# Head norms of a two-branch decoder layer: sums of squares by a transposing reduce on VectorE instead of one-row matmuls on TensorE

## The chip, the core and the metric

The kernel runs on one NeuronCore of one Trainium2 chip. The metric is the device time of one execution in microseconds (us). TensorE (PE) multiplies matrices into PSUM; VectorE (DVE), ScalarE (ACT) and GpSimd (POOL) do elementwise work; SyncE (SP) issues nearly all DMAs, in program order.

## The reference, cut to what matters

One layer on 2048 positions of width 1024, all in float32. A combined input projection feeds a short convolution branch (1024 channels, 8 heads of 128) and a gated linear recurrence (1024 channels, 16 heads of 64). The step that changes is the norm of each head:

```python
def headwise_rms_norm(y, n_heads, g):
    b, s, d = y.shape
    yh = y.reshape(b, s, n_heads, d // n_heads)
    yh = yh * lax.rsqrt(jnp.mean(yh * yh, axis=-1, keepdims=True) + RMS_EPS)
    return yh.reshape(b, s, d) * g
...
    xn = rms_norm(h, ln_g)
    proj = jnp.einsum('bsd,de->bse', xn, w_in)
    b_gate, c_gate, x_conv, g_conv, x_lru, g_lru = jnp.split(proj, splits, axis=-1)
    y_conv = headwise_rms_norm(short_conv_mixer(...), N_CONV_HEADS, conv_out_g) * silu(g_conv)
    y_lru = headwise_rms_norm(rg_lru_mixer(...), N_LRU_HEADS, lru_out_g) * silu(g_lru)
    h = h + jnp.einsum('bse,ed->bsd', jnp.concatenate([y_conv, y_lru], -1), w_out)
    return rms_norm(h, final_g)
```

## The kernel before, in words

**Steps.** Channels lie on the 128 partitions and positions along the free axis. Positions are done in two halves of 1024, `h` = 0 and 1. A half has 24 steps: for each of 8 blocks of 128 channels a step "l" (recurrence), "a" and "b" (convolution). I call three such steps a triple. Then come 16 output steps "o". A step multiplies a 2x2 block of matrices by seven products instead of eight, each split into a high and a low part: seven groups of 4 x 3 matmuls of 128x128 by 128x512, all from line 886 into `bank` tiles in PSUM. The left factors are the tiles `s`, seven of them deep (`sset`, bufs=7). The first half makes them from `w_in` and stores them in HBM (`sd<-s`); the second half loads them (`s<-sd`). The output steps' factors (`so`) are made during the second half by a side job, described below, and loaded later (`s<-so`).

**Order.** The order on each engine is the order of the program's text, in slots: a slot is one product group, `tick()` opens it, and `at(n, f)` queues `f` for n slots later. Every engine works through its own queue in order, and SP does too. Each DMA instruction of SP also waits until the DMA eight places ahead of it on SP has landed, since eight semaphores are used in turn; the order's rows on waits show it below.

**What finishes a block.** `finish` gets a block's output `y` (tile `r` of the recurrence, tile `t` of the convolution, 128x1024) and its gate `sil` (tiles `gl`, `gb`). It multiplies them and stores the product (`yd<-gl`, `yd<-gb`). For the norm, ACT squares `y` in place (line 579), ACT copies it to the high part `qh` (line 581), and DVE subtracts to get the low part `ql` (line 160, the helper `tt`). Three slots later `head_sums` gives PE four matmuls, for two runs of 512 positions and two parts, each with a 128x64 slice of `sel` that has ones in one or two columns: they add one block's sums over channels to one or two rows of `norm_ps`, a PSUM tile into which all 16 blocks of a half accumulate. I call these four a quad; there are 32 of them. After the last, `head_norms` takes the square root (ACT), the reciprocal (DVE), and stores the 24 rows for each run of 512 positions into `rsd` with two DMAs.

**Who reads it.** `load_z` loads `yd` (`raw<-yd`) and the factors spread over partitions (`zr<-rsd`), and DVE multiplies them (`raw<-raw,zr`). The output steps need it for all positions. The side job `jobs()` starts with the third triple of the second half and does it for six of the output factors: it loads, multiplies, and writes seven pieces `so` each; in between it also prepares sums of `w_out` (`traw<-in_w_out_dram`, `td<-traw`). It makes one piece per slot, where `may()` allows it:

```python
    def may():
        p = place[0]
        if 8 <= p <= 12:
            return False
        return hlc[0] < (2 if p >= 20 or p <= 2 else 4)
```

`hlc` counts how many of the four `hl` tiles are taken; `qh` and `ql` are two of them, from two slots behind a block's `finish` to seven behind it. `gl` and `gb` take turns in two buffers (`o2`): DVE can't write the next one before the store of the last but one has landed.

Of the kernel before, what the change touches and what calls it, by code (L numbers as in the profile page):

```python
# [38 lines left out]
def hymba_kernel(ctx: ExitStack, tc: tile.TileContext, x, xt, w_in, par, lamc, w_gate, w_out, final_g, out):  # L39
# [51 lines left out]

    sel = const.tile([P, 3 * R], F32R, name="sel")
    nc.gpsimd.memset(sel.bitcast(F32), 0.0)
    nc.gpsimd.memset(sel.bitcast(F32)[:, R:R + 1], 1.0)
    nc.gpsimd.memset(sel.bitcast(F32)[:64, 2 * R:2 * R + 1], 1.0)
    nc.gpsimd.memset(sel.bitcast(F32)[64:, 2 * R + KT:2 * R + KT + 1], 1.0)

    inv_hd = const.tile([R, 1], F32, name="inv_hd")
    nc.vector.memset(inv_hd, 1.0 / 64)
# [197 lines left out]
    def load_z(h, m, zr, wait):  # L297
        r = [piece("raw") for _ in range(4)]
        fs = []
        for i in range(2):  # L300
# [4 lines left out]
            for q in range(2):
                zz = r[2 * i + q].rearrange("p (k t) -> p k t", k=NB)
                zq = z2[:, q * C:(q + 1) * C] if zr else piece("zr")
                k0 = (1 - h) * KT + q * NB
                nc.sync.dma_start(zz, yd[c][b, :, k0:k0 + NB, :])
                zq = zq.rearrange("p (k t) -> p k t", k=NB)  # L310
                if h == 1:
                    nc.sync.dma_start(zq, rsd[c][b:b + 1, k0:k0 + NB, :].broadcast_to((P, NB, P)))
                else:
                    nc.sync.dma_start(zq[:64], rsd[c][b:b + 1, k0:k0 + NB, :].broadcast_to((64, NB, P)))
# [225 lines left out]
    def head_norms(h):  # L540
        rs = aux("hn")[:R]
        nc.scalar.activation(out=rs, in_=norm_ps[0], func=AF.Sqrt, scale=inv_hd, bias=eps[:R])
        at(1, lambda: nc.vector.reciprocal(out=rs, in_=rs))

        def store():
            for i in range(2):
                nc.sync.dma_start(rsd[2 * h + i].rearrange("b h t -> h b t"),
                                  rs[32 * i:32 * i + 3 * KT, :].rearrange("h (b t) -> h b t", b=NB))
# [4 lines left out]
    def head_sums(h, qh, ql, col, row):
        if norm_ps[1] == 0:
            norm_ps[0] = psn.tile([P, C], F32, tag="norm", name="norm_ps")[:R]
        for i in range(2):
            s0 = col - (32 * i + row)
            for q in (qh, ql):
                nc.tensor.matmul(norm_ps[0], sel[:, s0:s0 + R], q[:, i * C:(i + 1) * C],  # L559
                                 start=norm_ps[1] == 0, stop=norm_ps[1] == 8 * KT - 1)  # L560
# [4 lines left out]

    def finish(d0, h, kt, y, sil, gain, col, row):
        v = {}

        def f1():
# [7 lines left out]

        def f2():
            nc.scalar.activation(out=y, in_=y, func=AF.Square)
            v["qh"], = hl_tile("qh")  # L580
            nc.scalar.copy(v["qh"], y)
# [702 lines left out]
```

## Time and profile before

| | |
|---|---|
| time, median of 3 runs | 1418.91 us (1418.45 to 1420.51) |
| span of the profiled execution, first to last instruction | 1418.1 us (the page gives no other time for it) |
| TensorE busy, matmuls | 94%, 5732 |
| VectorE / ScalarE / GpSimd busy | 75% / 55% / 17% |
| granted TensorE clock, mean | 0.981 |
| DMA moved | 371.02 MB, mean 262 GB/s |

Matmuls are pipelined, so the duration of one is longer than its share of the stream: what it costs is the distance from its start to the next one's start. "Idle before, releaser" in a row tells how long the engine stood still and which instruction ended that. By stages: a prologue to about 107 us, the first half to about 600, the second half to about 1120, and the output steps to the end.

### The profile page before, as it was taken

The page shows a single profiled execution, that of the slowest core. Times are in us where ns is not written, and L with a number is a line of the kernel's source. Part 1 is how long each engine was busy: PE and PEld are TensorE (multiplying, and loading weights), DVE is VectorE, ACT ScalarE, POOL GpSimd, SP SyncE. Part 2 cuts the span into 40 slices and gives each one's busy share as a digit, 9 for nine tenths or more (in the row PEclk, how much of TensorE's full clock was granted, in tenths as well). Part 3 has the DMA queues.
Part 4 walks back from the last instruction along what each step waited for, and adds up shares of the span by engine and source line. Part 5 has one row for each costly group of instructions (what it writes and reads, how often), then busy time and mean ns, then how long its engine had stood idle before and what let it go on. Part 6 is the DMA issues. An engine that isn't in the chain of part 4 may idle for free.

```text
span 1418.1 us, 16977 instructions
## 1 busy us (share of the span) xinstructions
PE 1336.5 (94%) x5732; PEld 1072.3 (76%) x5732; DVE 1069.9 (75%) x1273; ACT 782.6 (55%) x1165; POOL 242.6 (17%) x159
## 2 busy tenths in 40 slices
PE   6989999999999997899998999998996999988997
PEld 5867777778777775677886878786874888867886
DVE  6778788898989989777767667665667647657885
ACT  7485757666566666375563645463656323343443
POOL 2104333433534430101000000101010000000000
PEclk9999999999999998999999999999997999999999
DMA  5147797898888865730899999998979998697643
GB/s 213 30 141 256 274 280 212 310 326 284 310 280 293 315 242 198 240 97 30 291 315 339 331 339 333 368 294 302 300 259 340 352 304 260 223 390 284 214 155 144
DMA packets 165191, 371.02 MB, mean 262 GB/s; under 512 B 17265, under 2 KB 52465, under 8 KB 165105
## 3 DMA queue, kind: packets, MB, share of 16 engines
q1 hardware_dynamic: 164816, 369.63, 76.3%
q8 instruction: 45, 0.74, 0.2%
q14 instruction: 42, 0.34, 0.1%
q10 hardware_dynamic: 288, 0.32, 0.1%
HBM read 224.45 MB, written 145.43 MB: 261 GB/s over the span
## 4 chain that ended last, share of the span: by engine, by line
PE 65%; DMA 13%; ACT 9%; DVE 8%; issue 3%; SPq 2%; POOL 0%; DVEq 0%; ACTq 0%; POOLq 0%
PE bank L886 60%; PE norm_ps L559 2%; DMA sd<-s 2%; ACT i L673 2%; ACT r L673 2%; PE gate L666 2%; DMA s<-so 2%; DVE s L160 2%; DVE tl L160 1%; DMA yd<-gl 1%; DMA zr<-rsd 1%; DVE traw L160 1%; DMA raw<-in_w_in_dram 1%; DMA traw<-in_w_out_dram 1%; DMA raw<-yd 1%
## 5 line engine op out<-in xcount | busy, mean ns | idle before, releaser
L886 PE MATMUL bank<-th,s 128*128 128x512 f32 x3608 | 1147.0, 395 | 41.5 <-DMA s<-so 9.8
L886 PEld LDWEIGHTS bank<-th,s 128*128 128x128 f32 x3608 | 685.3, 190 | 204.4 <-ACT u L1223 12.2
L886 PE MATMUL bank<-tl,s 128*128 128x512 f32 x1804 | 710.5, 394 | 6.3 <-DVE tl L160 6.0
L886 PEld LDWEIGHTS bank<-tl,s 128*128 128x128 f32 x1804 | 342.9, 190 | 81.4 <-DVE tl L160 10.4
L160 POOL TENSOR_TENSOR s<-raw,s 128x512 fp32r<-128x512 f32 x62 | 118.9, 1931 | 256.4 <-ACT s L197 180.2
L197 ACT CAST s<-raw 128x512 fp32r<-128x512 f32 x136 | 81.8, 616 | 59.6 <-PE bank L886 43.4
L1223 ACT COPY u<-bank 128x512 f32<-128x512 f32 x58 | 34.0, 587 | 141.3 <-PE bank L886 90.9
L160 DVE TENSOR_TENSOR s<-s,s 128x512 fp32r<-128x512 f32 x102 | 103.5, 1015 | 5.4 <-ACT s L197 5.4
L160 DVE TENSOR_TENSOR tl<-traw,th 128x512 fp32r<-128x512 f32 x102 | 70.0, 711 | 47.5 <-ACT th L454 29.1
L160 POOL TENSOR_TENSOR gb<-gb,sg 128x1024 f32<-128x1024 f32 x16 | 41.8, 2611 | 351.4 <-ACT sg L599 331.4
L160 DVE TENSOR_TENSOR s<-raw,s 128x512 fp32r<-128x512 f32 (+1 forms) x120 | 89.8, 771 | 9.9 <-ACT s L197 5.3
L1220 ACT COPY q<-bank 128x512 f32<-128x512 f32 x58 | 33.8, 583 | 79.2 <-PE bank L886 74.2
L160 DVE TENSOR_TENSOR raw<-raw,zr 128x512 f32<-128x512 f32 x64 | 49.6, 801 | 29.6 <-DMA zr<-rsd 29.6
L197 ACT CAST s<-s 128x512 fp32r<-128x512 f32 x102 | 62.8, 616 | 5.9 <-DVE s L160 5.9
L640 DVE SCALAR_TENSOR_TENSOR u<-xl,pt,u 128x1024 f32<-128x1024 f32 x48 | 64.5, 1344 | 0.8 <-ACT u L636 0.2
L1226 ACT COPY rr<-bank 128x512 f32<-128x512 f32 x58 | 33.9, 584 | 47.8 <-PE bank L886 47.7
L160 DVE TENSOR_TENSOR st<-u,st 64x1024 fp32r<-64x1024 f32 x32 | 52.0, 1626 | 1.0
L750 DVE SCALAR_TENSOR_TENSOR t<-p,pt,t 128x1024 f32<-128x1024 f32 x32 | 47.6, 1486 | 4.9 <-ACT t L747 4.1
L160 POOL TENSOR_TENSOR gl<-gl,sg 128x1024 f32<-128x1024 f32 x16 | 45.8, 2862 | 20.1 <-ACT sg L599 20.1
L160 DVE TENSOR_TENSOR ob<-bank,rr 128x512 f32<-128x512 f32 x18 | 12.2, 689 | 48.0 <-ACT rr L1226 48.0
L636 ACT ACTIVATE u<-xl,pt 128x1024 f32<-128x1024 f32 x16 | 19.9, 1245 | 46.8 <-DVE xl L160 46.8
L673 ACT ACTIVATE r<-gate,pt 64x512 f32<-64x512 f32 x64 | 43.8, 684 | 2.4 <-PE gate L666 1.8
(162 smaller groups left out, 1355.9 us busy)
## 6 DMA issues: line engine op xcount, KB each, us to landing
sd<-s SPq DMA_DIRECT2D x147, 512.0 KB, 4.8
s<-sd SPq DMA_DIRECT2D x147, 512.0 KB, 5.9
raw<-in_w_in_dram SPq DMA_DIRECT2D x108, 256.0 KB, 5.0
so<-so SPq DMA_DIRECT2D x42, 512.0 KB, 6.0
s<-so SPq DMA_DIRECT2D x42, 512.0 KB, 7.5
raw<-yd SPq DMA_DIRECT2D x64, 256.0 KB, 5.4
traw<-in_w_out_dram SPq DMA_DIRECT2D x56, 256.0 KB, 5.9
yd<-gl SPq DMA_DIRECT2D x32, 256.0 KB, 3.6
```

What stands on the lines that cost most here:

```text
L160: (eng or nc.vector).tensor_tensor(out=out, in0=a, in1=b, op=op)
L197: nc.scalar.copy(dst[i][0], val(i))
L559: nc.tensor.matmul(norm_ps[0], sel[:, s0:s0 + R], q[:, i * C:(i + 1) * C], start=norm_ps[1] == 0, stop=norm_ps[1] == 8 * KT - 1)
L636: nc.scalar.activation(out=v["u"], in_=o1[:, 1:1 + N2], func=AF.Identity, scale=lw[0], bias=pt[:, LB + k:LB + k + 1])
L640: nc.vector.scalar_tensor_tensor(out=v["u"], in0=o1[:, 1 + j:1 + j + N2], scalar=lw[j], in1=v["u"], op0=ALU.mult, op1=ALU.add)
L666: nc.tensor.matmul(ps[j], v["gw"][n][:, j, :], v["st"][j][:, sl], start=(n == 0), stop=(n == 1))
L673: nc.scalar.activation(out=g_[hi, sl], in_=v["ps"][j][src], func=AF.Sigmoid, bias=pt[src, bias + k:bias + k + 1])
L750: nc.vector.scalar_tensor_tensor(out=tcur["t"], in0=p[:, 2 + j:2 + j + N2], scalar=cw[j], in1=tcur["t"], op0=ALU.mult, op1=ALU.add)
L886: nc.tensor.matmul(bank, a[:, js], b, start=start and n == 0, stop=stop and n == 2, skip_group_check=more)
L1220: nc.scalar.copy(q1, bk["A"])
L1223: nc.scalar.copy(u2, bk["A"])
L1226: nc.scalar.copy(rr, bk["A"])
```

## The change: one reduce per block, four short matmuls per half

The high and low parts, and the quads, go. After the square, DVE adds over channels in one `tensor_reduce` with `apply_transpose`: it reads the 1024 positions of a block as 32 runs of 32, in steps of 32 elements, transposes each 32x32 square of channels and positions, and adds along what were 32 channels. For each block it writes 32 columns of one PSUM tile `sums`: partition 32g+a, column r has the sum over channel group g at position 32a+r. When 16 blocks are done, `head_norms` splits `sums` into a high and a low part (`rt`), and four matmuls of 128x96 by 128x256 join two groups (heads of 64) or four (heads of 128). Root and reciprocal work on 96x256 instead of 64x512. The layout of the result is another one, so 24 DMAs of 4 partitions store it, in place of 2. `rsd` is laid out by halves.

```diff
-R = 64
+R = 32
+NR = 3 * R
...
-    rsd = [dram.tile([NB, 3 * KT, P], F32, name=f"rsd{c}") for c in range(NC)]
+    rsd = [dram.tile([2, NB, 3 * KT, P], F32, name=f"rsd{h}") for h in range(2)]
...
+    sel = [const.tile([P, NR], F32R, name=f"sel{n}") for n in range(2)]
...
     def head_norms(h):
-        rs = aux("hn")[:R]
-        nc.scalar.activation(out=rs, in_=norm_ps[0], func=AF.Sqrt, scale=inv_hd, bias=eps[:R])
-        at(1, lambda: nc.vector.reciprocal(out=rs, in_=rs))
+        sm_ = sums[0]
+        rt, = hl_tile("rt")
+        rh, rl = rt[:, 0:C], rt[:, C:2 * C]
+        at(4, lambda: hl_done(1))
+        v = {}
+
+        def split():
+            nc.scalar.copy(rh, sm_)
+            tt(rl, sm_, rh.bitcast(F32), ALU.subtract)
+
+        def add():
+            v["ps"] = pss.tile([P, C], F32, tag="s", name="norm_ps")[:NR, 0:KT * R]
+            parts = [(n, q) for n in range(2) for q in (rh, rl)]
+            for m, (n, q) in enumerate(parts):
+                nc.tensor.matmul(v["ps"], sel[n], q[:, (1 - n) * KT * R:(2 - n) * KT * R],
+                                 start=m == 0, stop=m == 3)
+
+        def root():
+            v["rs"] = aux("hn")[:NR, 0:KT * R]
+            nc.scalar.activation(out=v["rs"], in_=v["ps"], func=AF.Sqrt, scale=inv_hd, bias=eps[:NR])
 
         def store():
-            for i in range(2):
-                nc.sync.dma_start(rsd[2 * h + i].rearrange("b h t -> h b t"),
-                                  rs[32 * i:32 * i + 3 * KT, :].rearrange("h (b t) -> h b t", b=NB))
+            for w in range(3):
+                k0 = (w + 1) % 3 * KT
+                for i in range(2):
+                    for b in range(NB):
+                        p0 = w * R + (i * NB + b) * 4
+                        nc.sync.dma_start(
+                            rsd[h][i, b, k0:k0 + KT, :].rearrange("k (q r) -> q k r", q=4),
+                            v["rs"][p0:p0 + 4].rearrange("q (k r) -> q k r", k=KT))
...
+        split()
+        at(2, add)
+        at(3, root)
+        at(4, lambda: nc.vector.reciprocal(out=v["rs"], in_=v["rs"]))
+        at(5, store)
-    def head_sums(h, qh, ql, col, row):
...
-        for i in range(2):
-            s0 = col - (32 * i + row)
-            for q in (qh, ql):
-                nc.tensor.matmul(norm_ps[0], sel[:, s0:s0 + R], q[:, i * C:(i + 1) * C],
-                                 start=norm_ps[1] == 0, stop=norm_ps[1] == 8 * KT - 1)
+    def head_sums(h, kt, y):
+        if summed[0] == 0:
+            sums[0] = psn.tile([P, 2 * KT * R], F32, tag="sums", name="sums")
+        nc.vector.tensor_reduce(out=sums[0][:, kt * R:(kt + 1) * R], in_=y.rearrange("p (a r) -> p r a", r=R),
+                                axis=mybir.AxisListType.X, op=ALU.add, apply_transpose=True)
...
-    def finish(d0, h, kt, y, sil, gain, col, row):
+    def finish(d0, h, kt, y, sil, gain):
...
-        def f2():
-            nc.scalar.activation(out=y, in_=y, func=AF.Square)
-            v["qh"], = hl_tile("qh")
-            nc.scalar.copy(v["qh"], y)
-
-        def f3():
-            v["ql"], = hl_tile("ql")
-            tt(v["ql"], y, v["qh"].bitcast(F32), ALU.subtract)
...
-        at(d0 + 2, f2)
-        at(d0 + 3, f3)
-        at(d0 + 6, lambda: head_sums(h, v["qh"], v["ql"], col, row))
-        at(d0 + 7, lambda: hl_done(2))
+        at(d0 + 2, lambda: nc.scalar.activation(out=y, in_=y, func=AF.Square))
+        at(d0 + 3, lambda: head_sums(h, kt, y))
```

The order on the engines, at three places. First DVE in a triple of the first half, where `r` and `t` are a block's output; before:

```order
L160 TENSOR_TENSOR gl<-bank,rr 128x512
L160 TENSOR_TENSOR ql<-r,qh 128x1024
L160 TENSOR_TENSOR s<-raw,s 128x512
...
L160 TENSOR_TENSOR raw<-raw 128x512
L160 TENSOR_TENSOR ql<-t,qh 128x1024
L160 TENSOR_TENSOR s<-s_2784,s 128x512
```

And after, at the same places:

```order
L163 TENSOR_TENSOR gl<-bank,rr 128x512
L586 TENSOR_REDUCE sums<-r 128x32
L163 TENSOR_TENSOR s<-raw,s 128x512
...
L163 TENSOR_TENSOR raw<-raw 128x512
L586 TENSOR_REDUCE sums<-t 128x32
L163 TENSOR_TENSOR s<-s_2734,s 128x512
```

The reduce stands exactly where the subtraction stood; nothing else moves on DVE in the first half.

Second, SP in the second half, from the third load of gate weights (`bd`, one in each triple) on; `so` is the side job's store, `traw` its load of `w_out`. Before:

```order
L612 DMA bd<-in_w_gate_dram 128x256
L575 DMA yd_86<-gb 128x4x128
L575 DMA yd_87<-gb 128x4x128
L218 DMA s<-sd_103 128x1024
L218 DMA s<-sd_104 128x1024 x6
L381 DMA traw<-in_w_out_dram 128x512 x4
L218 DMA s<-sd_104 128x1024
L218 DMA s<-sd_105 128x1024
L422 DMA so_120<-so 128x1024
L218 DMA s<-sd_105 128x1024
L422 DMA so_120<-so 128x1024
```

After:

```order
L626 DMA bd<-in_w_gate_dram 128x256
L385 DMA traw<-in_w_out_dram 128x512 x4
L600 DMA yd_86<-gb 128x4x128
L600 DMA yd_87<-gb 128x4x128
L426 DMA so_118<-so 128x1024
L221 DMA s<-sd_101 128x1024
L221 DMA s<-sd_102 128x1024
L426 DMA so_118<-so 128x1024
L221 DMA s<-sd_102 128x1024 x5
L426 DMA so_118<-so 128x1024
L399 DMA td_127<-traw 128x512 x4
```

With two `hl` tiles no longer taken, `may()` says yes more often, and the side job runs ahead. Counted over the order's rows from one load of `bd` to the next, second half, triple by triple:

| loads of `bd` | 3rd to 4th | 4th to 5th | 5th to 6th | 6th to 7th | 7th to 8th | from the 8th on |
|---|---|---|---|---|---|---|
| `so` stores, before / after | 7 / 9 | 7 / 9 | 7 / 8 | 7 / 7 | 7 / 7 | 5 / 0 |
| `traw` loads | 8 / 12 | 8 / 8 | 8 / 8 | 4 / 0 | 0 / 0 | not the job's |
| `td` stores | 8 / 8 | 8 / 12 | 8 / 8 | 4 / 0 | 0 / 0 | 0 / 0 |
| `raw<-yd` loads | 4 / 4 | 4 / 4 | 4 / 8 | 4 / 4 | 4 / 0 | not the job's |

Third, SP in the output steps, where the factors of the second half are stored. Before:

```order
L218 DMA s<-so_122 128x1024 x3
L547 DMA rsd_90<-hn 24x4x128
L547 DMA rsd_91<-hn 24x4x128
L819 DMA od_138<-xr 128x1024
L218 DMA s<-so_122 128x1024
L218 DMA s<-so_123 128x1024 x2
L309 DMA raw<-yd_86 128x512
L314 DMA zr<-rsd_90 64x512
```

After:

```order
L221 DMA s<-so_120 128x1024 x2
L572 DMA rsd_89<-hn 4x8x32 x24
L221 DMA s<-so_120 128x1024
L833 DMA od_136<-xr 128x1024
L221 DMA s<-so_120 128x1024
L221 DMA s<-so_121 128x1024 x2
L313 DMA raw<-yd_86 128x512
L318 DMA zr<-rsd_89 64x512
```

The same place with the waits of each row, after:

```order
L221 DMA s<-so_120 128x1024 [waits DMAHW4_49,PE_49]
L572 DMA rsd_89<-hn 4x8x32 [waits DMAHW5_49,DVE_49]
L572 DMA rsd_89<-hn 4x8x32 [waits DMAHW6_49]
L572 DMA rsd_89<-hn 4x8x32 [waits DMAHW7_49]
L572 DMA rsd_89<-hn 4x8x32 [waits DMAHW0_49]
...
L221 DMA s<-so_120 128x1024 [waits DMAHW5_49,PE_49]
```

The store has moved one slot ahead, and 24 DMAs take turns on eight semaphores, so each waits for the one eight places ahead; four loads `s<-so` and the loads of `yd` and `rsd` stand behind them.

More of the change, by code (lines that the diff above doesn't have):

```diff
@@ L89, in hymba_kernel @@
     nc.scalar.activation(out=warm, in_=eps, func=AF.Exp)
[L92 to L99, printed above, removed]
-    for i in range(2):
-        nc.vector.memset(inv_hd[32 * i:32 * i + KT, :], 1.0 / 128)
+    sel = [const.tile([P, NR], F32R, name=f"sel{n}") for n in range(2)]
+    for n in range(2):
+        nc.gpsimd.memset(sel[n].bitcast(F32), 0.0)
+    quarter = [ident[:, g * R:(g + 1) * R] for g in range(P // R)]
+    for w in range(2):
+        nc.gpsimd.tensor_tensor(out=sel[0][:, w * R:(w + 1) * R], in0=quarter[2 * w],
+                                in1=quarter[2 * w + 1], op=ALU.add)
+    nc.gpsimd.tensor_tensor(out=sel[1][:, 2 * R:], in0=sel[0].bitcast(F32)[:, 0:R],
+                            in1=sel[0].bitcast(F32)[:, R:2 * R], op=ALU.add)
+    inv_hd = const.tile([NR, 1], F32, name="inv_hd")
+    nc.vector.memset(inv_hd[:2 * R], 1.0 / 64)
+    nc.vector.memset(inv_hd[2 * R:], 1.0 / 128)
     hx = const.tile([P, KT, 4], F32, name="hx")
@@ L301, in load_z @@
             c, b = divmod(2 * m + i, NB)
-            assert c < 2 or normed
+            assert normed[c // 2]
+            rs_ = rsd[c // 2][c % 2]
             zz_, zq_ = [], []
@@ L311, in load_z @@
                 if h == 1:
-                    nc.sync.dma_start(zq, rsd[c][b:b + 1, k0:k0 + NB, :].broadcast_to((P, NB, P)))
+                    nc.sync.dma_start(zq, rs_[b:b + 1, k0:k0 + NB, :].broadcast_to((P, NB, P)))
                 else:
-                    nc.sync.dma_start(zq[:64], rsd[c][b:b + 1, k0:k0 + NB, :].broadcast_to((64, NB, P)))
+                    nc.sync.dma_start(zq[:64], rs_[b:b + 1, k0:k0 + NB, :].broadcast_to((64, NB, P)))
                     k0 += KT
-                    nc.sync.dma_start(zq[64:], rsd[c][b:b + 1, k0:k0 + NB, :].broadcast_to((64, NB, P)))
+                    nc.sync.dma_start(zq[64:], rs_[b:b + 1, k0:k0 + NB, :].broadcast_to((64, NB, P)))
                 fs.append(lambda zz=zz, zq=zq: tt(zz, zz, zq, ALU.mult))
@@ L534, in second_half @@
                 at(free.pop(1) - 7, lambda c=c, kt=kt: cols(c, kt))
-    norm_ps = [None, 0]
-    normed = []
+    normed = [False, False]
+    sums, summed = [None], [0]
     def head_norms(h):
-        rs = aux("hn")[:R]
-        nc.scalar.activation(out=rs, in_=norm_ps[0], func=AF.Sqrt, scale=inv_hd, bias=eps[:R])
-        at(1, lambda: nc.vector.reciprocal(out=rs, in_=rs))
-        def store():
-            for i in range(2):
-                nc.sync.dma_start(rsd[2 * h + i].rearrange("b h t -> h b t"),
-                                  rs[32 * i:32 * i + 3 * KT, :].rearrange("h (b t) -> h b t", b=NB))
-            normed.extend([h] * h)
-        at(3, store)
@@ L553, in head_sums @@
-    def head_sums(h, qh, ql, col, row):
-        if norm_ps[1] == 0:
-            norm_ps[0] = psn.tile([P, C], F32, tag="norm", name="norm_ps")[:R]
-        for i in range(2):
-            s0 = col - (32 * i + row)
-            for q in (qh, ql):
-                nc.tensor.matmul(norm_ps[0], sel[:, s0:s0 + R], q[:, i * C:(i + 1) * C],
-                                 start=norm_ps[1] == 0, stop=norm_ps[1] == 8 * KT - 1)
-                norm_ps[1] += 1
-        if norm_ps[1] == 8 * KT:
-            norm_ps[1] = 0
+        sm_ = sums[0]
@@ new lines, in head_norms @@
+        split()
[8 more added lines that the diff above has]
+                                axis=mybir.AxisListType.X, op=ALU.add, apply_transpose=True)
+        summed[0] += 1
+        if summed[0] == 2 * KT:
+            summed[0] = 0
```

6 lines of the change are left out of this document (3 added, 3 removed).

## The prediction

> **What bounds the kernel now.** I read the page's busy shares first, then windows cut at the triples, then the timeline of TensorE around one quad, then the waits, and last DMA and SP. Columns of a window: length, busy us and count for PE, PEld, DVE, ACT and POOL, granted clock, DMA share, GB/s.
>
> ```profile
> PE 1336.5 (94%) x5732; PEld 1072.3 (76%) x5732; DVE 1069.9 (75%) x1273; ACT 782.6 (55%) x1165; POOL 242.6 (17%) x159
> 436.50:499.10 62.60, 61.85 (x270) 49.67 (x269) 57.29 (x58) 40.51 (x59) 25.60 (x15) 1.00 0.85 296
> 580.50:710.80 130.30, 128.75 (x564) 104.55 (x563) 92.09 (x106) 75.89 (x102) 14.19 (x8) 1.00 0.51 168
> 710.80:778.40 67.60, 63.40 (x275) 50.45 (x274) 45.26 (x52) 33.17 (x45) 5.91 (x4) 1.00 0.97 328
> 778.40:844.60 66.20, 63.42 (x270) 50.58 (x269) 45.39 (x52) 33.39 (x45) 5.92 (x4) 0.97 0.95 335
> 844.60:909.30 64.70, 61.84 (x270) 49.69 (x269) 45.21 (x52) 33.47 (x45) 5.91 (x4) 1.00 0.98 343
> 909.30:972.20 62.90, 59.07 (x257) 47.11 (x256) 39.55 (x46) 31.47 (x42) 6.27 (x4) 1.00 0.97 323
> 972.20:1033.70 61.50, 61.24 (x269) 49.47 (x268) 38.98 (x44) 33.36 (x45) 6.79 (x4) 1.00 0.88 292
> 1033.70:1120.00 86.30, 75.46 (x304) 58.43 (x303) 58.30 (x71) 48.44 (x70) 8.18 (x4) 0.90 0.85 310
> ```
>
> The second row is a triple of the first half: PE is full, and DVE is nearly full, 57.3 of 62.6 us. In the second half the same triple takes 67.6 down to 61.5 us. Where it takes most, DMA is busy 0.95 to 0.98 of the time; where DMA is at 0.88, it takes least. So three limits lie close together: PE everywhere, DVE in the first half, DMA from 711 to 972 us.
>
> **Quads removed.** Columns from here on: start, duration, engine, line, instruction.
>
> ```profile
> 311.18 0.39 PE L559 MATMUL norm_ps<-qh,sel 128*64 128x512 f32 x1
> 311.41 0.39 PE L559 MATMUL norm_ps<-ql,sel 128*64 128x512 f32 x1
> 311.64 0.40 PE L559 MATMUL norm_ps<-qh,sel 128*64 128x512 f32 x1
> 311.88 0.39 PE L559 MATMUL norm_ps<-ql,sel 128*64 128x512 f32 x1
> 312.11 0.39 PE L886 MATMUL bank<-th,s 128*128 128x512 f32 x1
> L559 PE MATMUL norm_ps<-ql,sel 128*64 128x512 f32 x64 | 25.7, 402 | 6.6 <-DVE ql L160 6.6
> ```
>
> A quad holds PE's stream for 312.11 - 311.18 = 0.93 us, and 32 of them for 29.8 us. Besides, PE stood 6.6 us before quads until `ql` came. The eight new matmuls have half the columns: at half of 0.23 us each, an estimate from these rows, 0.5 us per half. If PE alone set the end, the kernel would gain 29.8 + 6.6 - 0.9 = 35.5 us. The stages give much of it back.
>
> **DVE: the reduce for the subtraction.** No row of the trace has a transposing reduce, nor an operand read in steps of 32 elements.
>
> ```profile
> L160 DVE TENSOR_TENSOR ql<-t,qh 128x1024 fp32r<-128x1024 f32 x16 | 22.8, 1422 | 0.0
> L160 DVE TENSOR_TENSOR ql<-r,qh 128x1024 fp32r<-128x1024 f32 x16 | 20.0, 1251 | 0.0
> L700 DVE TENSOR_TENSOR_SCAN r<-r,hl,u 128x1024 f32<-128x1024 f32 x8 | 18.8, 2350 | 0.2
> L543 DVE RECIPROCAL hn<-hn 64x512 f32<-64x512 f32 x2 | 6.7, 3334 | 0.0
> 320.62 1.76 DVE L160 TENSOR_TENSOR ql<-t,qh 128x1024 fp32r<-128x1024 f32 x1
> 306.19 1.22 DVE L160 TENSOR_TENSOR ql<-r,qh 128x1024 fp32r<-128x1024 f32 x1
> DVE xx L160 <- PE bank L886: 2.3, 1, 2.3
> DVE u L160 <- ACT i L673: 0.8, 1, 0.8
> DVE gb L160 <- ACT rr L1226: 0.7, 1, 0.7
> DVE gl L160 <- ACT rr L1226: 0.5, 1, 0.5
> DVE s L160 <- ACT s L197: 0.5, 1, 0.5
> PE bank L886 <- DVE tl L160: 5.8, 5, 4.0
> L581 ACT CAST qh<-t 128x1024 fp32r<-128x1024 f32 x16 | 16.8, 1051 | 0.7 <-PE norm_ps L559 0.3
> ```
>
> The low end is 1.2 us, the subtraction itself: one element after the other. The high end is twice the reciprocal's 3.3 us for 512 elements, 6.7 us. I take 2.35 us, the scan's: it is the nearest row of a 1024-element pass that is slower than plain streaming, and each element of the reduce lies 128 bytes from the last. The Trainium skill, "Advanced Engine Details and Errata", section Memory Cachelines, says that an access to another 16-byte line each time is penalised in SBUF; no run here shows it, and it gives no factor. Against it, the Trainium skill, "VectorE: DVE Perf Modes", section The perf-mode tier table, has `tensor_reduce` at the plain one-element rate; no run here shows it, and by it the sum would be that of the low end. I give the low end 0.4.
>
> In a triple of the first half two subtractions go (1.22 + 1.76 = 3.0 us) and two reduces come (4.7 us): DVE 57.3 + 1.7 = 59.0 us. Of DVE's 5.3 us idle, the 2.3 us for PE can go, while some 2 us of waiting for ACT's results stay (the four rows on waits for ACT). DVE then needs about 61.1 us, and PE 62.6 - 1.9 = 60.7. So DVE sets the triple: a gain of 1.5 us instead of 1.9. From 107 to 499 us, 6.3 triples, that is -9 us (bounds: -12 to -15 with a 1.2 us reduce, where DVE needs 58.7 us and its last waits for PE's sake go too; 0 with one of 3.15 us). At the turn of the halves, 499 to 580 us, PE waits 5.8 us for weights `tl` that DVE splits, with a `ql` in that chain: three quads gained, 2.8 us, two longer reduces lost, 2.2 us: -0.5 us.
>
> ACT loses 32 casts of 1.05 us (line 581). I cost that at nothing: ACT is busy 40.5 of 62.6 us in the triple, so it mostly waits.
>
> **Second half: the side job runs ahead.** From 580 to 711 us DMA has room (0.51): four quads, -3.7 + 0.5 = -3 us. Then the change moves DMA work forward. The GB/s times the lengths give 22.2 MB in each of the three windows from 710.8 to 909.3 us.
>
> ```profile
> so<-so SPq DMA_DIRECT2D x42, 512.0 KB, 6.0
> traw<-in_w_out_dram SPq DMA_DIRECT2D x56, 256.0 KB, 5.9
> raw<-yd SPq DMA_DIRECT2D x64, 256.0 KB, 5.4
> DVE gl L160 <- DMA yd<-gl: 31.4, 6, 6.3
> 835.14 0.69 DVE L160 TENSOR_TENSOR gl<-bank,rr 128x512 f32<-128x512 f32 x1 [6.26 <-DMA yd<-gl]
> ```
>
> By the counts of the order, two `so` and four `traw` (or `td`) are added in the first and in the second of them, 2.1 MB each, and one `so` with a whole `load_z` (about 2.1 MB) in the third, 2.6 MB: 66.5 MB become 73.3. The last two rows show how a busy DMA reaches PE: the store of `gl` lands late, DVE stands 6.3 us for its buffer, and what is queued behind it, bank evacuations too, comes late. At the mean rate of the three windows, 335 GB/s, 73.3 MB take 219 us, against 198.5 now; at the rate of the best one with the share raised from 0.98 to 1.03, 360 GB/s, 203 us. If the added bytes were hidden, 198.5 - 5.6 for six quads - 3 for waits on `ql` = 190 us. I take 204.5: +6 us (bounds -9 and +14). Afterwards the work is missing: the window from 909.3 comes down to about PE's 60, the next one too: -2.9 - 1.5 = -4.5 us. From 1033.7 to 1120 us:
>
> ```profile
> PE bank L886 <- DMA s<-so: 7.1, 4, 2.9
> ```
>
> Three quads, -2.8; five `so` stores fewer, 2.6 MB or 8 us of DMA at 310 GB/s, in the place where PE waits for `s<-so`: I take -4 of the 7.1 us (bounds 0 and -7).
>
> **24 stores instead of 2.**
>
> ```profile
> L547 SPq DMA_DIRECT2D rsd<-hn x4: 312/338/363, 602.4 to 1129.4; - x4
> s<-so SPq DMA_DIRECT2D x42, 512.0 KB, 7.5
> 1129.06 0.73 SPq L547 DMA_DIRECT2D rsd<-hn  x2
> 1130.58 5.71 SPq L218 DMA_DIRECT2D s<-so  x3
> 1136.38 0.38 SPq L309 DMA_DIRECT2D raw<-yd  x1
> 1136.85 0.46 SPq L314 DMA_DIRECT2D zr<-rsd  x1
> ```
>
> On SP 24 issues at about 0.37 us (two in 0.73) are 9 us. With eight in flight, the first wait for big loads ahead to land (7.5 us), and two more rounds follow: 9 to 14 us before SP goes on. Behind them stand four `s<-so` and the `zr<-rsd` that need these stores. A tile `s` is reloaded six groups, 6 x 2.7 us = 16 us (12 matmuls of 0.23 us each group), before its use: 14 us late plus 7.5 us to land overshoots by some 5, 9 us late by nothing. I take +3 us in the output steps (bounds 0 and +12), with 0.5 for the short matmuls. At 602 us the window around it has DMA at 0.51, and I take 0.
>
> **Sum.** -9 - 0.5 - 3 + 6 - 4.5 - 6.8 + 3.5 = -14 us against the profiled span of 1418.1 us; the median, 1418.91, is 0.8 us above it, so about 1405. DVE's waits on ACT, 2.5 us in a triple, may shrink with ACT's shorter queue, for which I take off 2 in all: 1403 us. A difference of 0.2% (2.8 us) is about what can be told from none here.
>
> **Rivals.** (1) *The transfers are hidden anyway.* The second half's middle takes 190 us: 15 us less, 1388. For it: single stretches with big packets do move more than the 335 GB/s mean. Against it: the share of 0.95 to 0.98 over 200 us, and triples that get shorter as DMA gets freer. Chance 0.2. (2) *The stores take the place of the quads.* SP stands 14 us while DMA is busy, DVE waits for `zr`, PE for banks: +12 instead of +3, 1412 us. For it: the in-order queue; against it: the 16 us of lead. Chance 0.1. (3) *VectorE becomes the bound and the kernel is slower.* A triple of the first half takes 56.3 us + two reduces. It reaches today's 62.6 at 3.15 us; since the other stages gain 4 us, or 0.6 per triple, the kernel is slower from 3.5 us on. At the reciprocal's price of 6.7 us a triple takes 69.7: 6.3 x 7.1 = 45 us lost, less the 4: about 1460. For it: DVE's 57 of 62.6 us; against it: an addition does no division. Chance 0.08. (4) *It does nothing*: DMA gives back +14 and the stores +8 at once, 1416 to 1421 us. Chance 0.07. The forecast itself has 0.55, between 1395 and 1411.
>
> Eight times in ten the time lies between 1387 and 1416: this holds the forecast and the rivals (1) and (2). Faster by over 0.2%: the forecast, (1), (2), less a little for its tail, 0.84; same 0.08; slower 0.08.
>
> **What would show it.** Right: no row of line 559 but eight short matmuls; the reduce at 2.2 to 2.5 us; triples of the first half near 61 us with DVE over 58 busy; the three windows after 711 us at a DMA share near 1.0 and not shorter than now; 1034 to 1120 us shorter by 5 or more. A reduce near 1.2 us would give triples of about 60.2 us and 3 to 6 us more gain. Wrong: DMA at 0.95 with triples at 61 us there (rival 1), or a hole in PE of over 5 us just after the 24 stores (rival 2).

## The result, and the profile after

The changed kernel takes 1406.68 us (median of 4, 1404.29 to 1412.66) against 1418.68 us for the kernel before on the same chip: a ratio of 0.9914, 95% interval 0.9888 to 0.994. So it is faster, by 0.6 to 1.1%; the forecast was 1403 us. The profiled execution took 1404.29 us and has a span of 1402.2 us. A second set of five runs gave 1402.94 us (1398.37 to 1405.47), 0.9883 [0.9867, 0.9899]. The changed kernel scatters by 7 to 8 us between executions. Every ratio in this document is against the kernel before on the same chip, whose medians there lie between 1418.7 and 1419.9 us, so times from different chips can be compared to about 1 us.

First the busy shares, then the costliest groups that are new, from the page and the groups by line (behind the first bar: busy us and mean ns of one; behind the second: idle us before them):

```profile
PE 1309.4 (93%) x5612; PEld 1056.3 (75%) x5612; DVE 1071.1 (76%) x1274; ACT 749.3 (53%) x1135; POOL 225.9 (16%) x160
L586 DVE TRANSPOSE_TENSOR_REDUCE sums<-t 128x32 f32<-128x1024 f32 x16 | 33.8, 2110 | 0.0
L586 DVE TRANSPOSE_TENSOR_REDUCE sums<-r 128x32 f32<-128x1024 f32 x16 | 33.4, 2090 | 0.0
L559 PE MATMUL norm_ps<-rt,sel 128*96 128x256 f32 x8 | 1.3, 282 | 0.0
```

PE lost 120 matmuls, 27 us of busy time and the 6.6 us of waits for `ql`. ACT lost 33 us. DVE kept its 1070 us. The reduce costs 2.1 us. Of PE's 34 us, 16 reached the end of this execution (12 by the medians).

To see where, I cut both traces at events that are the same work in both: ACT's row `T<-r,nklam`, once per triple; the first `ob<-bank,q` of the output steps; the first `ob<-ob,rs,fg`, seven output steps later. Columns as in the prediction's windows. Before:

```profile
91.67:532.66 440.99, 431.80 (x1871) 346.28 (x1871) 390.73 (x393) 293.68 (x429) 168.97 (x101) 1.00 0.83 281
532.66:615.85 83.19, 68.53 (x265) 51.24 (x265) 63.73 (x80) 46.69 (x66) 6.72 (x4) 0.92 0.60 209
615.85:738.61 122.76, 122.40 (x537) 99.61 (x537) 87.20 (x101) 72.09 (x100) 14.14 (x8) 1.00 0.56 181
738.61:936.01 197.40, 187.57 (x805) 149.76 (x805) 135.76 (x154) 100.29 (x133) 17.76 (x12) 0.99 0.97 337
936.01:1108.67 172.66, 157.91 (x660) 124.57 (x660) 115.28 (x137) 96.95 (x132) 17.73 (x9) 0.95 0.87 300
1108.67:1285.71 177.04, 168.41 (x726) 137.76 (x725) 107.74 (x150) 56.24 (x97) 0.00 (x0) 0.98 0.90 309
1285.71:1418.07 132.36, 125.19 (x548) 103.22 (x546) 102.44 (x151) 56.95 (x111) 0.00 (x0) 0.98 0.56 185
```

After:

```profile
91.53:527.35 435.82, 421.27 (x1816) 340.88 (x1815) 383.04 (x393) 279.43 (x414) 154.10 (x101) 0.99 0.84 284
527.35:608.16 80.81, 65.81 (x261) 49.97 (x261) 64.31 (x81) 44.85 (x66) 6.69 (x4) 0.92 0.59 209
608.16:728.83 120.67, 119.49 (x521) 97.13 (x521) 95.07 (x108) 69.16 (x97) 12.55 (x8) 1.00 0.58 201
728.83:929.58 200.75, 185.53 (x782) 148.74 (x781) 145.12 (x164) 95.22 (x130) 18.65 (x12) 0.97 0.97 355
929.58:1087.25 157.67, 149.46 (x641) 120.56 (x641) 106.34 (x120) 87.41 (x121) 16.02 (x9) 0.99 0.86 290
1087.25:1271.24 183.99, 170.01 (x728) 137.40 (x727) 107.69 (x151) 56.50 (x98) 0.00 (x0) 0.98 0.86 297
1271.24:1402.23 130.99, 123.57 (x546) 101.98 (x544) 102.41 (x151) 56.97 (x111) 0.00 (x0) 0.99 0.56 187
```

The stages are: seven triples of the first half; the turn; two triples before the side job; three with it at its densest ("the middle"); the rest of the second half; seven output steps; the end. The sizes foreseen are for the prediction's own cuts (107, 499, 580, 711, 909 and 1120 us), so they fit these stages only roughly.

| stage | before | after | second profile of after | foreseen |
|---|---|---|---|---|
| first half | 441.0 | 435.8 (-5.2) | 433.4 (-7.6) | -9 |
| turn | 83.2 | 80.8 (-2.4) | 82.0 (-1.2) | -0.5 |
| two triples | 122.8 | 120.7 (-2.1) | 121.0 (-1.8) | -3 |
| middle | 197.4 | 200.8 (+3.4) | 200.4 (+3.0) | +6 |
| rest of the second half | 172.7 | 157.7 (-15.0) | 156.8 (-15.9) | -11.3 |
| seven output steps | 177.0 | 184.0 (+7.0) | 180.8 (+3.7) | +3.5 |
| end | 132.4 | 131.0 (-1.4) | 131.0 (-1.4) | 0 |

Read alone, this table confirms the prediction almost line by line. The experiments show that two of its lines are right for a wrong reason.

### The profile page after: what moved, and what is told of

Same layout as the page of the kernel before. It is cut to its first block, busy times and chain, and to the rows that moved or that the text cites. A ratio compares the mean times of both kernels' runs of the same rounds, so it can differ in the third digit from the quotient of the medians.

```text
span 1402.2 us, 16765 instructions
## 1 busy us (share of the span) xinstructions
PE 1309.4 (93%) x5612; PEld 1056.3 (75%) x5612; DVE 1071.1 (76%) x1274; ACT 749.3 (53%) x1135; POOL 225.9 (16%) x160
## 4 chain that ended last, share of the span: by engine, by line
PE 43%; DMA 19%; DVE 14%; ACT 6%; issue 6%; SPq 2%; POOL 1%; DVEq 0%; ACTq 0%; POOLq 0%
PE bank L900 42%; DMA s<-so 3%; DMA zr<-rsd 3%; DVE s L163 3%; DMA sd<-s 3%; DMA yd<-gl 2%; DVE sums L586 2%; PE gate L680 2%; ACT i L687 2%; ACT r L687 1%; DMA traw<-td 1%; DMA so<-so 1%; DVE u L654 1%; DMA raw<-in_w_in_dram 1%; DMA s<-sd 1%
## 5 line engine op out<-in xcount | busy, mean ns | idle before, releaser
L163 POOL TENSOR_TENSOR s<-raw,s 128x512 fp32r<-128x512 f32 x62 | 110.3, 1791 | 251.3 <-ACT s L200 221.1
L163 DVE TENSOR_TENSOR s<-s,s 128x512 fp32r<-128x512 f32 x102 | 88.9, 871 | 7.9 <-ACT s L200 7.9
L163 DVE TENSOR_TENSOR s<-raw,s 128x512 fp32r<-128x512 f32 (+1 forms) x120 | 85.0, 731 | 10.0 <-ACT s L200 5.3
L163 DVE TENSOR_TENSOR raw<-raw,zr 128x512 f32<-128x512 f32 x64 | 44.5, 721 | 29.7 <-DMA zr<-rsd 29.6
L654 DVE SCALAR_TENSOR_TENSOR u<-xl,pt,u 128x1024 f32<-128x1024 f32 x48 | 62.3, 1297 | 2.0 <-ACT u L650 1.5
L163 DVE TENSOR_TENSOR st<-u,st 64x1024 fp32r<-64x1024 f32 x32 | 45.5, 1422 | 1.0
L680 PE MATMUL gate<-st,bh 128*128 128x512 f32 x64 | 28.9, 452 | 16.7 <-DVE st L163 6.8
L687 ACT ACTIVATE i<-gate,pt 64x512 f32<-64x512 f32 x64 | 43.8, 684 | 1.1
```

The lines of the kernel that those rows point to most:

```text
L163: (eng or nc.vector).tensor_tensor(out=out, in0=a, in1=b, op=op)
L654: nc.vector.scalar_tensor_tensor(out=v["u"], in0=o1[:, 1 + j:1 + j + N2], scalar=lw[j], in1=v["u"], op0=ALU.mult, op1=ALU.add)
L680: nc.tensor.matmul(ps[j], v["gw"][n][:, j, :], v["st"][j][:, sl], start=(n == 0), stop=(n == 1))
L687: nc.scalar.activation(out=g_[hi, sl], in_=v["ps"][j][src], func=AF.Sigmoid, bias=pt[src, bias + k:bias + k + 1])
```

## Experiments: the pace of the side job

**The changed kernel again**, as the control for the runs beside it.

> The changed kernel once more, beside the next three on the same chip. All theories: 1404 to 1410 us, output steps of the first sixteen-row block 184 us long from the first to the second phase.

1402.94 us, as told above (span 1396.3): a little under what was expected, and with 180.8 us for the output steps instead of 184.

**The old pace.** By pace I mean how many pieces the side job makes in each triple. `may()` is the only link between the removed `hl` tiles and the order on SP. So the count alone is put back:

```diff
         at(d0 + 3, lambda: head_sums(h, kt, y))
+
+        def take(n):
+            hlc[0] += n
+
+        at(d0 + 2, lambda: take(1))
+        at(d0 + 3, lambda: take(1))
+        at(d0 + 7, lambda: take(-2))
```

> The changed kernel, with the count of taken hl tiles raised and lowered in the slots where qh and ql used to be taken, so that the side job keeps its old pace; nothing else differs. Theory (DMA is the limit in the middle of the second half, and the side job that runs ahead ate the gain): the three triples after 711 us go from 200.7 us to 188-193, the stretch from 909 us to the output steps, 157.7 us now, gets 6 to 10 us longer, total 1402 to 1409. Rival (the transfers are hidden, the 200.7 us have another cause, such as the granted clock of 0.95 there): the three triples stay at 199 to 202 and the later stretch at 157 to 160, total 1404 to 1409.

1424.00 us (1417.77 to 1431.12), 1.0037 [1.0022, 1.0052]: 21 us slower than the changed kernel, and slower than the kernel before. Neither theory gave this. The middle and the rest of the second half:

```profile
725.16:929.56 204.40, 187.79 (x781) 150.56 (x781) 137.23 (x154) 93.88 (x127) 18.40 (x12) 0.96 0.93 326
929.56:1105.69 176.13, 154.84 (x641) 122.00 (x640) 118.89 (x137) 90.63 (x126) 16.39 (x9) 0.95 0.85 294
```

The middle has no quads, moves the bytes that it moved before, and takes 204.4 us: not the 188 to 193 of my theory, and 7 us more than with the quads. The rest of the half takes 176 us, 20 more than at the new pace. So the side job that runs ahead did not eat the gain; it is where the gain is. The DMA share of 0.93 to 0.97 did not mean that DMA could do no more: at the new pace the middle moves 355 GB/s instead of 326 to 337, in less time than here.

**PE alone.** The kernel before, with only the last block's quad of each half; 15 of 16 blocks are left out of the sums.

```diff
+        if norm_ps[1] < 8 * KT - 4:
+            norm_ps[1] += 4
+            return
-        if norm_ps[1] == 0:
+        if norm_ps[1] == 8 * KT - 4:
...
```

> The kernel before, with the quad of the last block of each half alone: 30 of 32 quads are left out, and so the sums of 15 of 16 blocks; casts, subtractions, pace of the side job and stores stay. It relieves PE and nothing else. Theory (three limits close together): triples of the first half 62.6 to 60.5-61.2 us, the three triples after 711 us from 197.4 to 192-197 since DMA holds them, total 1395 to 1404. Rival (PE alone sets the end): all 28 us of the quads and 6 us of waits for ql are gained, 1383 to 1389.

1412.54 us, 0.9948 [0.9934, 0.9962]: 7 us for 30 quads that hold PE's stream for 28: neither theory had so little. Its steady triple of the first half, where 62.6 us should have become 60.5 to 61.2, and its windows of the middle and the rest of the second half:

```profile
406.09:468.37 62.28, 60.40 (x262) 48.41 (x261) 57.42 (x58) 40.49 (x59) 25.41 (x15) 1.00 0.86 298
732.29:933.28 200.99, 186.47 (x782) 149.56 (x781) 132.03 (x154) 100.13 (x133) 17.73 (x12) 0.97 0.96 331
933.28:1106.19 172.91, 155.40 (x642) 123.25 (x641) 115.33 (x137) 96.83 (x132) 17.02 (x9) 0.94 0.86 300
```

When the middle starts, it is 6.3 us ahead of the kernel before (732.3 against 738.6), the old-pace kernel 13.4 us (725.2). When the output steps start, the three stand at 1108.7, 1106.2 and 1105.7 us. At the old pace, then, what is gained ahead of the side job is nearly all lost in it; taking PE's work out there gained nothing in these executions.

The rows show part of the reason. In the middle this kernel has 23 matmuls fewer than the kernel before, but PE's busy time falls by 1.1 us only, not by 5, and the granted clock is 0.97 instead of 0.99. One quad of the middle, before:

```profile
770.78 0.45 PE L559 MATMUL norm_ps<-ql,sel 128*64 128x512 f32 x1 [1.43 <-DVE ql L160]
775.84 0.50 PE L886 MATMUL bank<-th,s 128*128 128x512 f32 x1 [1.40 <-ACT q L1220]
767.00:780.00 13.00, 10.18 (x44) 7.59 (x43) 10.96 (x14) 3.83 (x4) 0.00 (x0) 1.00 0.97 353
```

And the same place without the quad:

```profile
770.51 0.80 PE L889 MATMUL bank<-th,s 128*128 128x512 f32 x1 [3.18 <-ACT q L1223]
770.20:773.60 3.40, 3.09 (x7) 2.49 (x8) 3.36 (x4) 2.02 (x3) 0.00 (x0) 0.51 0.89 309
```

Before, PE stands 1.43 us for `ql`, does the quad, stands 1.40 us for `q`, and the granted clock stays at 1.00. Without the quad it stands 3.18 us at once, and goes on at half the clock. This happens once in each triple of the middle (3.14 to 3.18 us; 3.98 to 4.01 us in the old-pace kernel). So the quads there stood inside a wait that is no shorter without them. That the longer stop brings the lower clock is read from the order of events; no run tests it by itself.

**What holds the triples at the old pace.** In these 350 us DVE waits for the store of a block's product to leave the buffer of `gl`: in the old-pace kernel 29.0 us in five waits. (Rows on waits give us in all, times, longest.) One triple of it, SP and DVE:

```profile
DVE gl L163 <- DMA yd<-gl: 29.0, 5, 6.6
738.73 1.27 DVE L595 SCALAR_TENSOR_TENSOR gl<-r,pt,gl 128x1024 f32<-128x1024 f32 x1
745.49 2.22 SPq L221 DMA_DIRECT2D s<-sd  x2
747.79 1.26 SPq L600 DMA_DIRECT2D yd<-gl  x2
756.46 0.69 DVE L163 TENSOR_TENSOR gl<-bank,rr 128x512 f32<-128x512 f32 x1 [5.58 <-DMA yd<-gl]
```

The product is ready at 740.0 us; SP, busy with the loads of the side job, issues its store at 747.8; DVE gets the buffer at 756.5. Two kernels bring the store forward at the old pace. The first, against the old-pace kernel, moves it one slot ahead in SP's order in the second half:

```diff
-        at(d0 + (1 if kt == KT and h == 0 else 2), store)
+        at(d0 + (1 if h == 1 or kt == KT else 2), store)
```

> The kernel with the side job's old pace (1424 us), with the store of a block's product yd one slot (2.7 us) earlier in SP's order in the second half; no byte more or less is moved. Theory (one chain sets these triples at the old pace: SP comes late to the store yd<-gl, DVE stands 5.6 us for the buffer of gl, and the next bank with it; PE's quads lay beside this wait): the wait for yd<-gl falls to 1-4 us, the five triples after 725 us from 66-69 to 63-66 us each, total 1407 to 1417. Rival (the bytes set them, DMA's share of 0.93): 66 to 69 us still, total 1421 to 1427.

1415.66 us (1407.92 to 1421.01), 0.9967 [0.9949, 0.9985]: 8 us less. The waits fall to 21.3 us in five, and the five triples from 337.9 to 329.9 us together: the total is the theory's, while the waits and the triples are at its upper ends or over them. The second also takes it off SP:

```diff
-                nc.sync.dma_start(yd[2 * h + i]...
+                (nc.sync, nc.scalar)[h].dma_start(yd[2 * h + i]...
```

> The changed kernel with the side job's old pace, and with the stores of yd in the second half on ACT's queue, one slot earlier; so they no longer stand behind the 12 loads of the side job in SP's queue (with the old pace gl was ready at 740.0 us, SP issued its store at 747.8, and DVE got the buffer at 756.4). No byte more or less is moved. Theory (SP's queue makes the store late, and the late store sets the triples at the old pace): the store goes out near 743, DVE's wait for yd<-gl falls from 5.6 us to 0-2.5, the five triples after 725 us go from 66-69 to 61-65 us, total 1400 to 1410. Rival (DMA itself sets them, and the store takes as much longer to land): waits of 4 us and more, triples of 65 to 68 us, total 1413 to 1424.

1416.94 us (1412.34 to 1422.51), 0.9985 [0.997, 1.0]: 7 us less: the wait is as the theory had it, the time as the rival had it. The five triples do take 323.7 us instead of 337.9, but 7 us of that come back in the two triples ahead of them (122.7 against 119.1) and in the last one (46.2 against 42.5). The wait is nearly gone, and others stand in its place. Waits of PE from 725 to 1106 us, first in the old-pace kernel, then in this one; last, DVE's wait in this one from 710 to 1060 us:

```profile
PE bank L907 <- ACT q L1241: 17.3, 5, 4.0
PE bank L907 <- DMA s<-sd: 3.4, 4, 1.4
```

```profile
PE bank L907 <- DMA s<-sd: 11.7, 8, 2.8
PE bank L907 <- ACT q L1241: 4.5, 3, 2.3
DVE gl L163 <- DMA yd<-gl: 4.5, 3, 2.1
```

PE no longer waits for banks behind the late buffer, but 8 us more for its factors. So the late store costs 7 to 8 us at the old pace; this is shown. The wait for it is no mark of the old pace, though: the changed kernel has 26.6 us of it in the same 350 us, and at the new pace an earlier store gains nothing (last run of the experiments on the factors' stores).

From the start of the middle to the output steps the old pace takes 380.5 us, the new one 358.4. By the rows of both, 14.5 of these 22 us are PE standing still, and 7.6 are the same number of matmuls taking longer, at a granted clock of 0.96 and 0.95 instead of 0.97 and 0.99. What makes the other 13 us of the pace is argued only: the old pace loads a whole `z` at the same place of each of five triples, and every DMA around it is late; the new pace has one triple without such a load, and five `so` stores fewer in the last stretch. No run separates these two.

## Experiments: VectorE

**The reduce in unit steps.**

```diff
-in_=y.rearrange("p (a r) -> p r a", r=R)
+in_=y.rearrange("p (r a) -> p r a", r=R)
```

> The changed kernel, with the reduce reading each partition's 1024 elements one after the other instead of in steps of 32; the sums then belong to positions in another order, so its output is not the reference's. Theory A (the 128-byte steps make it 2.1 us): the reduce takes 1.2 us, DVE's busy time in a triple of the first half falls from 56.5 to about 54.7 us, the triple from 60.9 to about 60.2, total 3 to 6 us less, 1400 to 1404. Theory B (the transposition itself makes two passes): 2.1 us as now, total 1404 to 1409.

```profile
L586 DVE TRANSPOSE_TENSOR_REDUCE sums<-t 128x32 f32<-128x1024 f32 x16 | 20.0, 1248 | 0.0
L586 DVE TRANSPOSE_TENSOR_REDUCE sums<-r 128x32 f32<-128x1024 f32 x16 | 20.0, 1248 | 0.0
```

The reduce is as theory A had it: the 128-byte steps cost 0.85 us of the 2.1, and the rest is what the subtraction `ql<-r,qh` of the same size took (1251 ns), so no price of the transposition shows. 1396.86 us, 0.9845 [0.9828, 0.9863]: 6 us less by the medians, though the profiled executions differ by 1.5 us alone (spans 1394.8 and 1396.3).

**The reduce twice**, in the first half: the call stands in a loop of two where `h == 0`.

> The changed kernel, with the reduce issued twice for each block of the first half. Theory (DVE is close to being the bound there: 56.5 us busy of 60.9, some 2 us of waits on ACT that stay): 4.2 us more work in a triple give triples of 62.5 to 64 us, total 10 to 18 us more, 1415 to 1424. Rival (PE sets the triple, DVE has 4.4 us to spare): triples of 60.9 to 61.5, total 1404 to 1410.

1424.94 us, 1.0034 [1.0022, 1.0047]: 18 and 22 us more than the two sets of the changed kernel, at the theory's upper end or over it. A steady triple of the first half, from one `T<-r,nklam` to the next, first in the changed kernel, then with unit steps, then with the reduce twice:

```profile
404.84:465.71 60.87, 59.83 (x262) 48.57 (x261) 56.32 (x58) 38.47 (x58) 23.46 (x15) 1.00 0.88 306
```

```profile
401.13:461.83 60.70, 59.86 (x262) 48.57 (x261) 56.08 (x58) 38.48 (x57) 23.23 (x15) 1.00 0.87 304
```

```profile
418.55:482.25 63.70, 60.70 (x262) 48.34 (x261) 59.33 (x60) 38.35 (x57) 23.09 (x15) 1.00 0.83 292
```

Taking 1.7 us of reduces out gains 0.2 us, where 0.7 was foreseen. But DVE's busy time fell by 0.24 us alone, since its subtractions got longer (last section), so this run did not relieve DVE as it was meant to. That PE sets the triple rests on its being busy 59.8 of 60.9 us. Putting 4.2 us in costs 2.8: by the price of the reduces DVE has some 1.4 us to spare, by its busy time (3.0 us more) only 0.2. The two are nearly in balance, as foreseen, but rather on PE's side.

## Experiments: the stores of the factors

**Three stores in place of 24.** `rsd` is turned round to channel rows first, so that 32 partitions fit one DMA (the readers' lines, changed to match, are left out):

```diff
-rsd = [dram.tile([2, NB, 3 * KT, P], F32, ...
+rsd = [dram.tile([3 * KT, 2, NB, P], F32, ...
...
+                nc.sync.dma_start(
+                    rsd[h][k0:k0 + KT].rearrange("k i b (q r) -> (i b q) k r", q=4),
+                    v["rs"][w * R:(w + 1) * R].rearrange("q (k r) -> q k r", k=KT))
```

> The changed kernel, with rsd laid out by channel row and then position, so that 3 stores of 32 partitions per half take the place of 24; the factors are then read in runs of 512 bytes instead of 2048. Theory (the 24 issues of 0.35 us on SP hold up the loads of yd and rsd and so the first output steps): the first phase of the output steps goes from 184 us to 177-179, total 1399 to 1402. Rival (the loss of 7 us there comes from elsewhere, the issues have time to spare): 182 to 184 us, total 1404 to 1408. Third: the shorter runs make the loads of the factors slower, which shows in the median landing time of zr<-rsd and gives 1406 to 1412.

1442.44 us, 1.0164 [1.015, 1.0178]: 40 us slower than the changed kernel. The third theory had the cause and a fifth of its size. DMA packets of the changed kernel (second profile) and of this one, then this one's loads of the factors (number, size of each, median us to landing), which took 5.2 and 5.6 us to land in the kernel before:

```profile
DMA packets 166485, 371.00 MB, mean 266 GB/s; under 512 B 18944, under 2 KB 53760, under 8 KB 166400
```

```profile
DMA packets 190965, 371.00 MB, mean 258 GB/s; under 512 B 18848, under 2 KB 86432, under 8 KB 190880
zr<-rsd SPq DMA_DIRECT2D x64, 128.0 KB, 7.2
zr<-rsd SPq DMA_DIRECT2D x32, 256.0 KB, 9.3
L163 DVE TENSOR_TENSOR raw<-raw,zr 128x512 f32<-128x512 f32 x64 | 43.2, 688 | 80.1 <-DMA zr<-rsd 80.0
```

DVE waits 80.0 us for these loads, 30.8 in the changed kernel's second profile. The same bytes in 24,480 more packets: the middle takes 223 us instead of 200. The issue of the stores is not answered by it. Two more kernels had this layout, and are read against 1442 us. With the old pace as well:

> The changed kernel with the old pace of the side job and 3 stores per half. Theory (pace moves time about and the 24 stores cost 5 to 7 us): 1398 to 1403 us. Rival (neither matters): 1404 to 1409.

1467.17 us, 1.0324 [1.0305, 1.0344]: 25 us more, about the pace's 21 once again. With the side job started one step earlier (`n == 3 * KT + 5` instead of `+ 6`):

> The changed kernel with 3 stores per half, and the side job started one step before the third triple of the second half instead of with it; it then stores seven so pieces in each triple from the second on, in place of 2, 9, 9, 8, 7, 7. Theory (DMA is the limit from 711 to 909 us and has room, share 0.50, before): the three triples go from 200.7 to 190-197 us, total 1390 to 1398. Rival (PE and DVE set these triples): 198 to 201, total the same as with 3 stores alone, 1399 to 1403.

1444.62 us, 1.0179 [1.0166, 1.0193]: no gain. The three middle triples went from 223.1 to 213.9 us, by as much as the theory had, but the triple before them went from 67.7 to 75.1, so most of it was only moved.

**Six stores, with the old layout.** The reduce reads in unit steps, and the join is turned round: `sums`, its columns put in the order of position blocks, channel rows and runs, is the stationary operand and `sel` the moving one. Positions then come out along the free axis, in runs of 32.

```diff
-                nc.tensor.matmul(v["ps"], sel[n], q[:, (1 - n) * KT * R:(2 - n) * KT * R],
-                                 start=m == 0, stop=m == 3)
...
+                        nc.tensor.matmul(v["ps"][:, o:o + (1 + t) * R], q[:, c0:c0 + P], s,
+                                         start=m == 0, stop=m == 1)
...
+                    nc.sync.dma_start(
+                        rsd[h][i, :, k0:k0 + KT, :].rearrange("b k (q a) -> b (k q) a", q=4),
+                        v["rs"][:, o:o + R])
```

> The changed kernel with the reduce reading in unit steps and the four short matmuls turned round: sums is the stationary operand and sel the moving one, eight matmuls of 32 or 64 columns, so that positions come back in order with channel rows and runs of 32 on the partitions; 6 stores of 128 partitions per half take the place of 24, with the same runs of 128 bytes, and rsd and its readers stay as they are. Against the unit-step kernel with 24 stores (1396.9 us; output steps' first phase 180.4 us). Theory (24 issues on SP cost 4 us and more there): 176 to 178 us, total 1391 to 1395. Rival (the issues cost nothing, something else, such as the state of the bank queue at that point, sets the phase): 179 to 184 us, total 1395 to 1400.

1389.64 us (1387.35 to 1391.54), 0.9784 [0.9767, 0.9801]: 2.2% faster than the kernel before and the best of all. The output steps' first part takes 176.4 us, against 180.4 with unit steps and 24 stores; the theory holds for this stage, and the total is 1 us better than it had; the other 3 us lie ahead of the output steps (1080.7 against 1083.4 us where they start), within what one execution differs from another. SP at this place and PE's wait for the output factors from 1080 to 1300 us, in the changed kernel and in this one:

```profile
1105.39 8.87 SPq L572 DMA_DIRECT2D rsd<-hn  x24
PE bank L900 <- DMA s<-so: 9.2, 5, 4.0
1129.21 0.69 DVE L163 TENSOR_TENSOR raw<-raw,zr 128x512 f32<-128x512 f32 x1 [8.50 <-DMA zr<-rsd]
```

```profile
1098.15 3.43 SPq L584 DMA_DIRECT2D rsd<-hn  x6
PE bank L912 <- DMA s<-so: 1.0, 1, 1.0
```

With 24 stores, `s<-so` and the loads of the factors stand behind 8.9 us of issues, with six behind 3.4. PE waits 9.2 us for the former (8.1 in the unit-step kernel with 24 stores), DVE once 8.5 us for the latter.

**The earlier store of `yd` on top of it**, at the new pace:

> The same with the store of yd one slot earlier in the second half, as a version that could beat both kernels. Theory (the wait for yd<-gl also holds the triples from 727 to 864 us, 67.5 and 69.5 us, at the new pace): 2 to 6 us less than with six stores alone, 1386 to 1392. Rival (there DMA is full, share 1.00, and the order of its work changes nothing): the same within 2 us.

1393.20 us, 0.9809 [0.9792, 0.9827]: no gain, rather 3.6 us more, 3.1 of it in the output steps of the profiled executions (179.5 against 176.4). DVE's wait for `yd<-gl` fell from 19.0 to 3.7 us, and the middle takes 202.0 instead of 200.7 us, at 351 and 353 GB/s. At the new pace an earlier store there changes nothing, as the rival had it. That DMA bounds the middle now is argued from its share of 0.97 and from these rates; the old pace showed that such a share is no proof, and no run moves fewer bytes.

## Why the prediction was right or wrong

*First half, -9 for 107 to 499 us.* Right for the steady triple (from 62.6 to 60.9 us, where I had 61.1), too much in sum (-5.2 and -7.6 over seven triples). The step "DVE sets the triple" was wrong for the changed kernel: I had 59.0 us busy and measured 56.3, and one of my signs, DVE over 58, did not come. The reduce was 2.1 us, below the 2.2 to 2.5 of another sign, and the 128x512 subtractions `s<-s,s` beside it got shorter. PE, busy 59.8 of 60.9 us, sets the triple as far as the rows show. The quads alone were not what made it long: without them and with the old DVE work it takes 62.3 us. Two triples early in the half gained nothing in the profiled execution.

*The reduce between 1.2 and 2.35 us.* I took the scan's row for the 128-byte steps, with 0.4 on the low end. The reason was the right one: in unit steps it takes 1.25 us. By the Trainium skill, "Advanced Engine Details and Errata", section Memory Cachelines, a new 16-byte line for each access is penalised; the runs agree, and give the factor it leaves out, 1.7 here (2.1 us against 1.25).

*Middle, +6.* It measured +3.4 and +3.0, and two of its three triples got longer. The working that failed is the other half of the step: "if the added bytes were hidden, ... 190 us". At the old pace it takes 204.4 us. I had read a DMA share of 0.95 to 0.98 as a limit on bytes, so that bytes added cost time and bytes kept out save it, and scaled the rate with the share (360 GB/s at 1.03). The runs show that at the old pace the triple waited for late transfers, with a rate to spare: more DMA queued earlier raised 337 to 355 GB/s at the same share of 0.97. The -5.6 for six quads failed too: without its quads the middle is no shorter (201.0 us against 197.4). Rival (1), that the transfers are hidden and the middle takes 190 us, falls with it.

*After the middle, -11.3 in the prediction.* Measured -15.0 and -15.9. By my sums the new pace cost 14.5 in the middle (190 to 204.5) and gave back some 5, a loss of about 10 us; measured, it gains 21. By the same sums the rest of the change, at the old pace, gained some 25; measured, it loses 5 (1424.0 against 1418.8). Two errors of about 30 us each cancelled, and the total came within 4 us. That is luck: a prediction that is right in sum has not shown its terms.

*The 24 stores, +3.5 with a bound of +12.* +7.0 and +3.7 for the seven output steps. "Nine us late by nothing" was too hopeful: the issues took 8.9 us, as worked out, with no waits for the eight semaphores among them, and six stores give 4 us back in that place. Rival (2) was the right mechanism at a third to a half of its price.

*ACT's casts at nothing.* No run tests them alone; ACT is busy 38 of 60.9 us in the steady triple. The old-pace kernel, which has no casts, starts the middle 7 us ahead of the kernel that lacks only the quads (725.2 against 732.3), and its steady triple takes 60.9 us against 62.3. So the casts and subtractions, with the waits between them, were together worth more in the first half than the 2 us that I took off.

*Rival (3), VectorE the bound.* Not at 2.1 us. By the kernel with the reduce twice, with 1.4 us to spare for two reduces, DVE would set the triple from 2.8 us on, and a triple would be as long as before at about 3.7, where I had worked out 3.15. This is an estimate from that one run.

## What to carry to other kernels

Before taking time off a busy engine, take it off alone and see whether the end moves: 30 quads, 28 us of TensorE, were worth 7. In the middle these quads stood inside another wait, and taking them out joined two short stops of TensorE into a long one. A freed buffer or count can change the order of transfers elsewhere, and here that was worth more than the work removed; with the count put back the change is a small loss. A DMA share near 1 is no proof of a full rate: the middle moved 337 GB/s and 355 GB/s at the same share of 0.97.

## What the runs showed of the hardware

- A transposing reduce of 128x1024 in float32 takes 1.25 us in unit steps and 2.1 us in steps of 128 bytes: in unit steps one element each 1.2 ns, transposition included.
- Loads spread over partitions in runs of 512 bytes instead of 2048 cost 40 us for 24,480 more packets. By the shares of the two pages (76.9% of 1396.3 us, 76.6% of 1437.8) each of the 16 engines was busy 28 us longer, 18 ns per packet, an estimate from these rows. The Trainium skill, "DMA: Bandwidth & Descriptors", section Specifications, puts the least transfer for line rate at 512 B; at that size these loads took 7.2 and 9.3 us to land where they took 5.2 and 5.6 in the kernel before, so for them it was not enough.
- The same 128x512 subtraction on DVE (`s<-s,s`) has a mean of 1250 ns in a triple of the kernel before, 983 in the changed one, 882 with the reduce twice. Over the whole trace of the kernel before, 79 of its 102 ran while POOL did nothing, and none of them took over 0.70 us; the other 23 ran beside a POOL instruction and took 2.16 us on average. So DVE's busy time is no sum of fixed prices, and 1.7 us of reduces taken out lowered it by 0.24 us.
- In the middle of the kernel without the quads, TensorE stands 3.18, 3.18 and 3.14 us, and behind each of these stops its granted clock is halved for 3.4 to 6.8 us. In the kernel before, stops of 1.43 and 1.40 us at the first of these places left it at 1.00.
